# A hybrid attention and scan layer: six convolution blocks moved into the paired products, small roots and decay rows moved to GpSimd

## The chip, the cores and the metric

The kernel runs on one core of one Trainium2 chip. The metric is the device time of one execution in microseconds (us); lower is better. The engines are TensorE (PE; PEld is its loading of weights), VectorE (DVE), ScalarE (ACT), GpSimd (POOL) and SyncE (SP), which here only issues transfers. Each engine has a queue of its own and works through it in order.

## The reference

It is one layer of a streaming encoder, in float32, for 1024 tokens of a new stream and 64 tokens of a running one (512 cached keys): a shared input projection of width 1024, a short causal convolution and a chunked state scan (32 heads, 4 groups), a differential attention (8 heads of 2 components) beside it, gates, an output projection, and a convolutional feed-forward part of width 2816.

```python
xn = _rmsnorm(x, p['norm_mix_w'])
proj = xn @ p['w_in']
z, xbc, dt_raw, q, k, v, gate_ssm, gate_att = jnp.split(proj, np.cumsum(IN_SIZES)[:-1].tolist(), axis=-1)
xbc_c, conv_new = _causal_dwconv(conv_past, xbc, p['ssm_conv_w'], p['ssm_conv_b'])
xbc_c = jax.nn.silu(xbc_c)
...
y_ssm, ssm_new = _ssd_scan(xs, dt, a_neg, bm, cm, ssm_past.reshape(b, G, E, P, N), chunk_len)
y_ssm = (y_ssm + p['ssm_d'].reshape(G, E)[..., None] * xs).astype(x.dtype).reshape(b, t, SSM_D_INNER)
y_ssm = y_ssm * jax.nn.silu(z)
...
o = _diff_attention(q, k, v, q_pos, k_pos, lam)
o = (_rmsnorm(o, p['subln_w']) * (1.0 - lambda_init)).reshape(b, t, ATT_V_WIDTH)
mix = jax.nn.sigmoid(gate_ssm) * (y_ssm @ p['w_branch_ssm']) + jax.nn.sigmoid(gate_att) * (o @ p['w_branch_attn'])
x = x + mix @ p['w_out']
h = _rmsnorm(x, p['norm_ffn_w']) @ p['w_up']
ha, hb = jnp.split(h, 2, axis=-1)
hc, ffn_new = _causal_dwconv(ffn_past, ha, p['ffn_conv_w'], p['ffn_conv_b'])
x = x + (jax.nn.silu(hc) * hb) @ p['w_down']
```

The two places inside that the change touches are these, from the attention and from the scan:

```python
p = jax.nn.softmax(s, axis=-1).reshape(b, ATT_HEADS, 2, nq, -1)
a = p[:, :, 0] - lam * p[:, :, 1]
...
acum = jnp.cumsum(dtc * a_neg, axis=1)
seg = acum[:, :, None] - acum[:, None, :]
decay = jnp.exp(jnp.where(causal[None, :, :, None, None], seg, -jnp.inf))
```

## The kernel before

All 1088 tokens lie along the free axis, in two halves of 544 and quarters of 272; features lie on the 128 partitions. A float32 product is made from three fast ones: each operand is split into a rounded part (hi) and the rest (lo), and hi times hi, lo times hi and hi times lo are added up in PSUM. The weights are split when they arrive: ScalarE writes hi, VectorE subtracts (L156 and L157 for plain blocks, L429 and L430 for paired ones).

A **plain block** is 128 output features, made by `project`: four chunks of 272 tokens, each 8 slices of the inner dimension times 3 products (L171 to L173). A **pair** is two blocks and all tokens, made by `in_pair` with 7 products of half-size matrices in place of 8: each has 2 quarters x 4 slices x 3 matmuls of 272 columns. The left factors (`left_parts`, `make_left`; sums of weight blocks on GpSimd, L573 among them) and the right ones (`parts`, sums of token halves) are made ahead. The 7 products pile up in PSUM banks, and ScalarE or VectorE move a pile out, VectorE by adding `u1` or `u2` (L710). `INPUT` is the order of the pairs: q and k, z, then four of the gates g; `done` treats each finished half row and sends it to memory.

The stages follow each other:
1. A start with the norm and the values, to 116 us of the span.
2. The **stage of pairs**, 20 pairs, to 554 us. Other work (rotations of q and k, the step sizes) runs beside it as generators of small jobs, which `take_turn` advances.
3. **Attention**, to 1104 us: 8 heads x 9 query tiles = 72 units of `attend`. Each unit has two score products (psc banks), reductions, two exponentials with sums (L1142), the inversion of the second sum (L1144) and its product with lambda and the first sum (L1145), one multiply-add of the two probability tiles (L1146), transposes (L1157), copies to SBUF, and the product with the values. After 9 units `head_out` normalises the head with a logarithm and an exponential on ScalarE. Between them `fill(ATT_STEPS)` puts in chunks of `stream()`, the plain blocks of `ORDER`: the convolution blocks (`conv_tiles`: four taps, of which L1019 is three, and a silu made from tanh, L1020 and L1021) and gates. One unit of the rate is 363 columns, and `settle(1)` keeps one unit open: the scores of the next unit stand ahead of the transposes of this one.
4. The **scan**, to 1476 us: 36 steps over 4 groups of 9 chunks. `ask` fetches the decay rows of a step, spread over 128 partitions, into a `bc` tile (4 of them), two steps ahead; `front` masks it on GpSimd (L1317), applies exponentials and a product; `back` multiplies and carries the state (GpSimd, L1345). The rest of `stream()` and the two first branch products fill in between, with side loads through `b_g` tiles (`BG` of them).
5. The last branch and the output projection, to 1684 us, and the feed-forward part, to the end.

The code states the order of most work, and a scheduler turns it into queues: `tc.issue_after` keeps an instruction behind another, `tc.high_priority(n)` lets one go ahead. A tile of a pool with n buffers waits until the tile n before it is no longer used.

Of the kernel before, what the change touches and what calls it, by code (L numbers as in the profile page):

```python
# [17 lines left out]
P = 128  # L18
# [33 lines left out]
BG = 8  # L52
# [18 lines left out]
ATT_STEPS = 1.12  # L71
# [4 lines left out]
def group(g):  # L76
    return 16 + g, 20 + g, *range(4 * g, 4 * g + 4)


ORDER = (("c", group(0)), ("g", (11, 10)), ("c", group(1)), ("g", (9, 8)), ("c", group(2)), ("c", group(3)), ("g", (3, 2)))  # L80
INPUT = [(k, i) for k in "qk" for i in range(4)] + [("z", i) for i in range(8)] + [("g", i) for i in (2, 3, 6, 7)]
# [9 lines left out]
def hybrid_layer(ctx: ExitStack, tc: tile.TileContext, xT, xt, prm, cst, rope, wvd, win, wbs, wba, wout, wup, wdn,  # L91
# [239 lines left out]
    def staged(name):  # L331
        return st.tile([P, 384], F32, name=name, tag="zr", bufs=ZR)
# [153 lines left out]
    def row(tag, name, dt=F32):  # L486
# [3 lines left out]
        w = {"ss": T}.get(tag, HT)  # L490
        return rows_r.tile([P, w], dt, name=name, tag=tag, bufs=IN_ROWS[tag])
# [128 lines left out]
    def blocks_of(n):  # L620
        kind, j = INPUT[n]
        return [win[FIRST_BLOCK[kind] + 2 * j + r] for r in range(2)]
# [23 lines left out]
    def in_pair(n):  # L646
# [16 lines left out]
        def to(r, c, s):  # L663

            if (r, c) not in out:
                out[r, c] = row("fp", "pre")
            a, w = O2[s], W2[s]
            return out[r, c][:, a : a + w]

        def done(r, c):  # L670
            cs = slice(HT * c, HT * (c + 1))
# [22 lines left out]
        for _ in range(14):  # L694
# [8 lines left out]
            else:  # L703
# [3 lines left out]
                if u is None:  # L707
                    seen["copy"] = S.copy(to(r, c, s), ps)
                else:
                    seen["read"] = V.tensor_tensor(out=to(r, c, s), in0=ps, in1=u[:, us], op=ALU.add)  # L710
# [340 lines left out]
    with (tc.tile_pool(name="ak", bufs=1) as ak, tc.tile_pool(name="at", bufs=1) as at,  # L1051
# [51 lines left out]
        def attend(h, i, tiles, o_t, ssq, s0):  # L1103
# [40 lines left out]
            V.reciprocal(sm[:n, 1:2], sm[:n, 0:1])  # L1144
            V.scalar_tensor_tensor(sm[:n, 1:2], sm[:n, 1:2], nlam[:n], s0[:n, i : i + 1], ALU.mult, ALU.mult)  # L1145
# [33 lines left out]
            act(po[:n, P : 2 * P], po[:n, :P], AF.Square, accum_out=ssq[:n, i : i + 1])  # L1179
            yield  # L1180

        def head_out(h, o_t, ssq, s0):
            ms, rs, t0, t1 = (at.tile([P, 9], F32, name=n, tag=n, bufs=2) for n in ("ms", "ors", "on0", "on1"))
            V.tensor_tensor(out=ms, in0=s0, in1=s0, op=ALU.mult)
            V.tensor_scalar(ms, ms, EPS * 128, None, ALU.mult)
            V.tensor_tensor(out=ms, in0=ms, in1=ssq, op=ALU.add)
            act(t0, ms, AF.Ln, scale=1.0 / 128)
            act(t0, t0, AF.Exp, scale=-0.5)
# [813 lines left out]
```

## Time and profile before

| | |
|---|---|
| timed, median of 3 runs | 2409.57 us (2406.24 to 2413.95) |
| profiled execution | 2400.86 us |
| its span, first to last record | 2399.1 us |
| mean granted clock | 0.998 |
| ScalarE, activations of the exponentials L1142 | x144, 106.0 us |
| transfers | 450.58 MB, mean 188 GB/s |

Busy time by stage, in us of VectorE, ScalarE, GpSimd and TensorE (attention and the scan are among the rows of the prediction):

| stretch of the span, us | TensorE | VectorE | ScalarE | GpSimd |
|---|---|---|---|---|
| 0 to 116, start and values | 111.97 | 64.49 | 61.19 | 0.20 |
| 116 to 554, pairs | 434.78 | 315.29 | 199.18 | 142.36 |
| 1476 to 1590, a branch | 112.62 | 73.67 | 46.03 | 0.00 |
| 1684 to 2154, feed-forward, up | 466.60 | 329.46 | 191.21 | 226.12 |
| 2154 to 2399.1, feed-forward, down | 236.70 | 175.92 | 95.21 | 97.78 |

The profiled execution's own time is below the fastest of the timed runs; it is one execution, and its trace is what all durations come from. A row of a group gives a line of the kernel, the engine, the operation, what it writes and reads, its shape and count, then its busy time and mean duration, and at the end the idle time of its engine just before, with what ended it. Rows of stretches give the busy time of each engine between two times of the span. The weights of a matmul load beside the matmul before it, so PEld's busy time isn't added to PE's.

### The profile page before, as it was taken

The page shows a single profiled execution, that of the slowest core. Times are in us where ns is not written, and L with a number is a line of the kernel's source. Part 1 is how long each engine was busy: PE and PEld are TensorE (multiplying, and loading weights), DVE is VectorE, ACT ScalarE, POOL GpSimd, SP SyncE. Part 2 cuts the span into 40 slices and gives each one's busy share as a digit, 9 for nine tenths or more (in the row PEclk, how much of TensorE's full clock was granted, in tenths as well). Part 3 has the DMA queues.
Part 4 walks back from the last instruction along what each step waited for, and adds up shares of the span by engine and source line. Part 5 has one row for each costly group of instructions (what it writes and reads, how often), then busy time and mean ns, then how long its engine had stood idle before and what let it go on. Part 6 is the DMA issues. An engine that isn't in the chain of part 4 may idle for free.

```text
span 2399.1 us, 48662 instructions
## 1 busy us (share of the span) xinstructions
PE 2376.1 (99%) x18661; PEld 2306.1 (96%) x18661; DVE 1725.5 (72%) x2953; ACT 1197.8 (50%) x2592; POOL 623.0 (26%) x683
## 2 busy tenths in 40 slices
PE   9999999999999999999999999999999999999999
PEld 9999999999999999999899889999999999999999
DVE  4678987646858768884789886646866766767866
ACT  6344454425656656665666674334533443353432
POOL 0032444220100000001222220013254554453343
PEclk9999999999999999999999999999999999999999
DMA  7873868426555444435988956664124424357975
GB/s 248 273 243 135 275 214 310 165 105 205 158 160 161 148 141 138 143 114 183 360 272 287 333 192 207 197 211 139 63 82 159 148 96 160 124 182 220 253 189 120
DMA packets 288202, 450.58 MB, mean 188 GB/s; under 512 B 35865, under 2 KB 178082, under 8 KB 287970
## 3 DMA queue, kind: packets, MB, share of 16 engines
q1 hardware_dynamic: 259058, 388.39, 49.0%
q0 software_dynamic: 10176, 25.50, 5.0%
q10 hardware_dynamic: 18736, 33.59, 3.9%
q8 instruction: 147, 2.41, 0.4%
q14 instruction: 85, 0.70, 0.1%
HBM read 294.86 MB, written 152.50 MB: 186 GB/s over the span
## 4 chain that ended last, share of the span: by engine, by line
PE 56%; DVE 3%; DMA 1%; issue 1%; ACT 1%; SPq 0%; DVEq 0%; ACTq 0%
PE mx L1639 13%; PE mx L1821 6%; PE mm L1639 5%; PE mm L171 4%; PE mm L173 4%; PE mm L172 4%; PE mx L173 3%; PE mx L171 3%; PE mx L172 3%; PE mm L1821 2%; PE yi L1328 1%; PE stp L1340 1%; PE ye L1334 1%; PE po L1177 1%; PE tr L1307 1%
## 5 line engine op out<-in xcount | busy, mean ns | idle before, releaser
L171 PE MATMUL mm<-b,w_hi 128*128 128x272 f32 x1376 | 409.2, 297 | 0.0
L173 PE MATMUL mm<-b,w_lo 128*128 128x272 f32 x1376 | 404.0, 294 | 0.0
L172 PE MATMUL mm<-b,w_hi 128*128 128x272 f32 x1376 | 403.8, 294 | 0.0
L171 PEld LDWEIGHTS mm<-b,w_hi 128*128 128x128 f32 x1376 | 259.4, 188 | 7.2 <-issue 4.9
L172 PEld LDWEIGHTS mm<-b,w_hi 128*128 128x128 f32 x1376 | 259.4, 189 | 6.2 <-issue 4.9
L173 PEld LDWEIGHTS mm<-b,w_lo 128*128 128x128 f32 x1376 | 258.9, 188 | 3.9 <-issue 3.1
L1639 PE MATMUL mx<-m,w_hi 128*128 128x272 f32 x776 | 149.3, 290 | 1.5 <-ACT m L429 1.3
L430 DVE TENSOR_TENSOR wh<-w_f,wh 128x512 fp32r<-128x512 f32 (+1 forms) x156 | 149.1, 956 | 0.0
L1639 PE MATMUL mx<-n,wh 128*128 128x272 f32 x1056 | 141.2, 288 | 1.2 <-DVE u L1666 1.2
L1639 PEld LDWEIGHTS mx<-n,wh 128*128 128x128 f32 x1056 | 135.7, 188 | 1.4 <-DVE u L1666 1.4
L1142 ACT ACTIVATE p_t<-sc,mx 128x512 f32<-128x512 f32 (+6 forms) x144 | 106.0, 739 | 58.7 <-DVE mx L1133 35.0
L171 PE MATMUL mx<-b,w_hi 128*128 128x272 f32 x416 | 122.5, 295 | 1.6 <-ACT w_hi L156 1.1
L1639 PEld LDWEIGHTS mx<-m,w_hi 128*128 128x128 f32 x776 | 121.9, 188 | 2.0 <-ACT m L429 1.5
L172 PE MATMUL mx<-b,w_hi 128*128 128x272 f32 x416 | 122.0, 294 | 0.0
L173 PE MATMUL mx<-b,w_lo 128*128 128x272 f32 x416 | 120.1, 291 | 0.2 <-DVE w_lo L157 0.2
L573 POOL TENSOR_TENSOR ws<-w_f 128x512 f32<-128x512 f32 (+1 forms) x51 | 69.2, 1356 | 195.0 <-DMA w_f<-in_win_dram 94.0
L1019 DVE SCALAR_TENSOR_TENSOR cc<-pre,par,cc 128x544 f32<-128x544 f32 (+1 forms) x144 | 111.2, 772 | 8.2 <-ACT cc L1017 6.9
L157 DVE TENSOR_TENSOR w_lo<-w_f,w_hi 128x1024 fp32r<-128x1024 f32 (+1 forms) x74 | 91.1, 1232 | 31.3 <-ACT w_hi L156 30.7
L1639 PE MATMUL mx<-m,w_lo 128*128 128x272 f32 x388 | 112.0, 289 | 0.0
L1648 ACT ACTIVATE cc<-pre,par 128x544 f32<-128x544 f32 (+1 forms) x44 | 37.2, 845 | 148.0 <-DVE pre L1683 147.0
L429 ACT CAST wh<-w_f 128x512 fp32r<-128x512 f32 (+1 forms) x156 | 95.3, 613 | 28.7 <-POOL w_f L579 7.9
L156 ACT CAST w_hi<-w_f 128x1024 fp32r<-128x1024 f32 (+1 forms) x74 | 77.5, 1049 | 51.5 <-PE mm L172 28.4
(472 smaller groups left out, 7123.4 us busy)
## 6 DMA issues: line engine op xcount, KB each, us to landing
w_f<-in_win_dram SPq DMA_DIRECT2D x40, 512.0 KB, 3.6
w_f<-in_wup_dram SPq DMA_DIRECT2D x80, 256.0 KB, 2.6
w_f<-in_win_dram SPq DMA_DIRECT2D x76, 256.0 KB, 3.2
bc<-a_sc SPq DMA_DIRECT2D x32, 512.0 KB, 6.7
b<-y_sc SPq DMA_DIRECT2D x24, 544.0 KB, 9.3
h_sc<-hb SPq DMA_DIRECT2D x44, 272.0 KB, 2.1
ht<-h_sc SPq DMA_DIRECT2D x22, 544.0 KB, 4.7
t_sc<-ht SPq DMA_DIRECT2D x22, 544.0 KB, 2.9
```

Source lines behind the costliest of these rows:

```text
L156: S.copy(hi, w)
L157: V.tensor_tensor(out=lo, in0=w, in1=hi, op=ALU.subtract)
L171: PE.matmul(ps, a_hi, b_hi, start=i == 0, stop=False)
L172: PE.matmul(ps, a_hi, b_lo, start=False, stop=False)
L173: PE.matmul(ps, a_lo, b_hi, start=False, stop=i == n - 1)
L429: S.copy(hi, src)
L430: V.tensor_tensor(out=lo, in0=src, in1=hi, op=ALU.subtract)
L573: G.tensor_tensor(out=s1, in0=q21, in1=q22, op=ALU.add)
L1019: V.scalar_tensor_tensor(cc[:, :m], pre[:, i : i + m], cw(i), cc[:, :m], ALU.mult, ALU.add)
L1142: act(p_t[:n, :nk], sc[c][:n, :nk], AF.Exp, bias=mx[:n, c : c + 1], accum_out=dst)
L1639: PE.matmul(ps, w[x][:, c], b[y][:, k], start=start and k == i == 0, stop=k == 3 and i == 2, skip_group_check=not start)
L1821: PE.matmul(ps, w[y][:, c], b[z][:, k], start=start and k == j == 0, stop=k == n - 1 and j == 2, skip_group_check=not start)
```

## The change

- **Pairs.** The convolution blocks 16, 20, 0, 1, 2 and 3 leave `ORDER` and become three pairs of kind "c" in `INPUT`, behind z6, z7 and the first gate. `to` places their halves in longer rows (`fx`, `fc`: 3 more columns at each side), so that one evacuation of a quarter becomes two where the two streams meet. A new generator, `convolved`, does for each half row what `conv_tiles` does (ScalarE the first tap, VectorE three), then one Silu on ScalarE, and sends the result from ScalarE's queue; it joins `running`, the jobs that `take_turn` advances. `ATT_STEPS` goes from 1.12 to 0.87.
- **Roots and inversions.** The inversion of the sum becomes a power of -1 on GpSimd, and its product with lambda and the first sum follows there. In `head_out` the sums and a power of -0.5 on GpSimd replace VectorE's steps and ScalarE's logarithm and exponential; the factor of 128 goes into `wsub`. The Square reads the copied output and writes a tile of its own.
- **Decay rows.** `ask` issues its transfer from GpSimd in place of SyncE. The tiles of `side` and `staged` are 272 columns wide in place of 384, and `BG` goes from 8 to 12.

```diff
-BG = 8
+BG = 12
...
-ATT_STEPS = 1.12
+ATT_STEPS = 0.87
...
-ORDER = (("c", group(0)), ("g", (11, 10)), ("c", group(1)), ("g", (9, 8)), ("c", group(2)), ("c", group(3)), ("g", (3, 2)))
-INPUT = [(k, i) for k in "qk" for i in range(4)] + [("z", i) for i in range(8)] + [("g", i) for i in (2, 3, 6, 7)]
+PAIRED = ((16, 20), (0, 1), (2, 3))
+ORDER = (("c", group(1)), ("g", (11, 10)), ("c", group(2)), ("g", (9, 8)), ("c", group(3)), ("g", (3, 2)))
+INPUT = [(k, i) for k in "qk" for i in range(4)] + [("z", i) for i in range(6)]
+INPUT += [("z", 6), ("c", 0), ("z", 7), ("c", 1), ("g", 2), ("c", 2)] + [("g", i) for i in (3, 6, 7)]
...
     def staged(name):
-        return st.tile([P, 384], F32, name=name, tag="zr", bufs=ZR)
+        return st.tile([P, QW], F32, name=name, tag="zr", bufs=ZR)
...
-    def row(tag, name, dt=F32):
+    def row(tag, name, dt=F32, more=False):
         if tag in ("fa", "fs", "fu"):
             w = {"fa": KT * P, "fs": 4 * P, "fu": HT}[tag]
             return rows_l.tile([P, w], dt, name=name, tag=tag, bufs=IN_ROWS[tag])
-        w = {"ss": T}.get(tag, HT)
-        return rows_r.tile([P, w], dt, name=name, tag=tag, bufs=IN_ROWS[tag])
+        w = {"ss": T, "fx": HT + 6, "fc": HT + 6}.get(tag, HT)
+        t = rows_r.tile([P, w], dt, name=name, tag=tag, bufs=IN_ROWS[tag])
+        return t if tag == "ss" or more else t[:, :HT]
...
     def blocks_of(n):
         kind, j = INPUT[n]
+        if kind == "c":
+            return [win[B_X + f] for f in PAIRED[j]]
         return [win[FIRST_BLOCK[kind] + 2 * j + r] for r in range(2)]
...
         def to(r, c, s):
             if (r, c) not in out:
-                out[r, c] = row("fp", "pre")
-            a, w = O2[s], W2[s]
-            return out[r, c][:, a : a + w]
+                out[r, c] = row("fx" if kind == "c" else "fp", "pre", more=kind == "c")
+            a, w, d = O2[s], W2[s], 3 if kind == "c" else 0
+            if kind == "c" and c == 1 and s == 1:
+                m = TP - HT - a
+                return [(0, out[r, c][:, d + a : d + a + m]), (m, out[r, c][:, d + a + m + 3 : d + a + w + 3])]
+            return [(0, out[r, c][:, d + a : d + a + w])]
+
+        def convolved(r, c):
+            t, f = out[r, c], PAIRED[j][r]
+            n, m = (HT, HT) if c == 0 else (TP - HT, HT + 3)
+            if c == 0:
+                G.memset(t[:, 0:3], 0.0)
+            else:
+                G.tensor_copy(t[:, 0:3], out[r, 0][:, HT : HT + 3])
+                G.tensor_copy(t[:, 3 + n : 6 + n], par[:, O_CS + 3 * f : O_CS + 3 * f + 3])
+                G.tensor_copy(conv_o[:, f, 0:3], t[:, n : n + 3])
+                G.tensor_copy(conv_o[:, f, 3:6], t[:, HT + 3 : HT + 6])
+            cc = row("fc", "cc", more=True)
+            cw = lambda i: col(O_CW + 4 * f + i)
+            with after("copy"):
+                act(cc[:, :m], t[:, :m], AF.Identity, bias=col(O_CB + f), scale=cw(0))
+            yield 1
+            for i in range(1, 4):
+                with after("read"):
+                    V.scalar_tensor_tensor(cc[:, :m], t[:, i : i + m], cw(i), cc[:, :m], ALU.mult, ALU.add)
+                yield 1
+            with after("root", "copy"):
+                seen["silu"] = act(cc[:, :m], cc[:, :m], AF.Silu, scale=2.0)
+            yield 1
+            rs = slice(P * f, P * (f + 1))
+            send(out=x_sc[rs, HT * c : HT * c + n], in_=cc[:, :n])
+            if c == 1:
+                send(out=x_sc[rs, TP:T], in_=cc[:, n + 3 : m])
         def done(r, c):
+            if kind == "c":
+                for x in {(0, 0): (0,), (1, 0): (0, 1), (0, 1): (1,), (1, 1): ()}[r, c]:
+                    running.append([1 + 3 * (r == 1 and x == 1), convolved(r, x)])
+                return
...
                 ps = pile(key, p, s, start)
-                if u is None:
-                    seen["copy"] = S.copy(to(r, c, s), ps)
-                else:
-                    seen["read"] = V.tensor_tensor(out=to(r, c, s), in0=ps, in1=u[:, us], op=ALU.add)
+                for o, t in to(r, c, s):
+                    w = t.shape[1]
+                    if u is None:
+                        seen["copy"] = S.copy(t, ps)
+                    else:
+                        seen["read"] = V.tensor_tensor(out=t, in0=ps[:, o : o + w], in1=u[:, O2[s] + o : O2[s] + o + w], op=ALU.add)
...
                 pr.append(p_t)
-            V.reciprocal(sm[:n, 1:2], sm[:n, 0:1])
-            V.scalar_tensor_tensor(sm[:n, 1:2], sm[:n, 1:2], nlam[:n], s0[:n, i : i + 1], ALU.mult, ALU.mult)
+            G.tensor_tensor(out=sm[:n, 1:2], in0=sm[:n, 0:1], in1=minus[:n, 9:10], op=ALU.pow)
+            G.tensor_scalar(sm[:n, 1:2], sm[:n, 1:2], nlam[:n], s0[:n, i : i + 1], ALU.mult, ALU.mult)
...
                 PE.matmul(po[:n, :P], a_t[b // 4][:kw, b % 4 * P : b % 4 * P + n], rhs, start=b == 0, stop=b == nb - 1)
             S.copy(o_t[:n, i], po[:n, :P])
-            act(po[:n, P : 2 * P], po[:n, :P], AF.Square, accum_out=ssq[:n, i : i + 1])
+            sq = at.tile([P, P], F32, name="sq", tag="sq")
+            act(sq[:n], o_t[:n, i], AF.Square, accum_out=ssq[:n, i : i + 1])
             yield
         def head_out(h, o_t, ssq, s0):
-            ms, rs, t0, t1 = (at.tile([P, 9], F32, name=n, tag=n, bufs=2) for n in ("ms", "ors", "on0", "on1"))
-            V.tensor_tensor(out=ms, in0=s0, in1=s0, op=ALU.mult)
-            V.tensor_scalar(ms, ms, EPS * 128, None, ALU.mult)
-            V.tensor_tensor(out=ms, in0=ms, in1=ssq, op=ALU.add)
-            act(t0, ms, AF.Ln, scale=1.0 / 128)
-            act(t0, t0, AF.Exp, scale=-0.5)
-            V.tensor_scalar(ms, ms, -0.5 / 128, None, ALU.mult)
-            V.tensor_tensor(out=ms, in0=ms, in1=t0, op=ALU.mult)
-            V.tensor_tensor(out=t1, in0=ms, in1=t0, op=ALU.mult)
-            V.scalar_tensor_tensor(rs, t1, 1.5, t0, ALU.add, ALU.mult)
+            ms, rs = (at.tile([P, 9], F32, name=n, tag=n, bufs=2) for n in ("ms", "ors"))
+            G.tensor_tensor(out=ms, in0=s0, in1=s0, op=ALU.mult)
+            G.tensor_scalar(ms, ms, EPS * 128, None, ALU.mult)
+            G.tensor_tensor(out=ms, in0=ms, in1=ssq, op=ALU.add)
+            G.tensor_tensor(out=rs, in0=ms, in1=minus[:, :9], op=ALU.pow)
             V.tensor_tensor(out=o_t[:, :8], in0=o_t[:, :8], in1=rs[:, :8].unsqueeze(2).to_broadcast([P, 8, P]), op=ALU.mult)
...
-        V.tensor_scalar_mul(wsub, par[:, O_SUB : O_SUB + P], 1.0 - LAMBDA_INIT)
+        V.tensor_scalar_mul(wsub, par[:, O_SUB : O_SUB + P], (1.0 - LAMBDA_INIT) * math.sqrt(128.0))
+        minus = at.tile([P, 10], F32, name="minus")
+        V.memset(minus, -0.5)
+        V.memset(minus[:, 9:10], -1.0)
...
             ch, h8 = (c + o) // P, slice(8 * g, 8 * g + 8)
             L = P if ch < 8 else TS
             bc = sin.tile([P, 8, P], F32, name="bc", tag="bc", bufs=4)
-            load(out=bc[:, :, :L], in_=a_sc[ch, h8, :L].unsqueeze(0).to_broadcast([P, 8, L]))
+            G.dma_start(out=bc[:, :, :L], in_=a_sc[ch, h8, :L].unsqueeze(0).to_broadcast([P, 8, L]))
             return bc
...
         def side():
-            return bs.tile([P, 384], F32, name="b_g", tag="b_g", bufs=BG)
+            return bs.tile([P, QW], F32, name="b_g", tag="b_g", bufs=BG)
```

In the stage of pairs, these are rows of VectorE at the last quarter of one pair and the start of the next, before (`mx` and `mm` are banks, `u1` and `u2` the running sums, `pre` the row of a result, `wh` and `w_lo` split left factors):

```order
L710 TENSOR_TENSOR pre_6637<-mx_6624,u1_6458 128x272
L710 TENSOR_TENSOR pre_6637<-mm_6641,u1_6458 128x272
L430 TENSOR_TENSOR wh_6655<-ws2_6588,wh_6655 128x512
L710 TENSOR_TENSOR pre_6670<-mx_6590,u2_6459 128x272
L430 TENSOR_TENSOR wh_6674<-w_f_1759,wh_6674 128x512
L710 TENSOR_TENSOR pre_6670<-mx_6609,u2_6459 128x272
L430 TENSOR_TENSOR wh_6690<-w_f_1758,wh_6690 128x512
L430 TENSOR_TENSOR w_lo_6712<-ws1_6587,w_hi_6711 128x512
```

After, the same place behind the first convolution pair:

```order
L751 TENSOR_TENSOR pre_6983<-mx_6900,u2_6767 128x272
L432 TENSOR_TENSOR wh_6985<-w_f_1759,wh_6985 128x512
L751 TENSOR_TENSOR pre_6983<-mx_6920,u2_6767 128x208
L751 TENSOR_TENSOR pre_6983<-mx_6920,u2_6767 128x64
L432 TENSOR_TENSOR wh_7005<-w_f_1758,wh_7005 128x512
L695 SCALAR_TENSOR_TENSOR cc_6989<-pre_6950,par_81,cc_6989 128x544 x2
L432 TENSOR_TENSOR w_lo_7026<-ws1_6896,w_hi_7025 128x512
L695 SCALAR_TENSOR_TENSOR cc_6989<-pre_6950,par_81,cc_6989 128x544
L695 SCALAR_TENSOR_TENSOR cc_7035<-pre_6983,par_81,cc_7035 128x547
L432 TENSOR_TENSOR w_lo_7026<-w_f_1759,w_hi_7025 128x512
L739 TENSOR_TENSOR u2_7010<-mx_7063,u1_7009 128x272
```

The evacuation at the seam of the two streams is two instructions, and the taps of the convolution (L695) stand among the splits (L432) and ahead of the next pair's evacuation (L739).

In attention, these are rows of VectorE where a unit of 1024 keys is followed by one of 128 keys (`sm` holds a unit's sums, `sc` the scores' bank, `mx` the maxima, `p_t` the probabilities, `pt` transposes), before:

```order
L1144 RECIPROCAL sm_10664<-sm_10664 128x1
L1145 SCALAR_TENSOR_TENSOR sm_10664<-sm_10664,nlam_7211,s0_10570 128x1
L1136 MEMSET sc_10752 64x2x64
L1146 SCALAR_TENSOR_TENSOR p_t_10682<-p_t_10682,sm_10664,p_t_10680 128x1024
L1137 TENSOR_REDUCE mx_10751<-sc_10752 128x2
L1144 RECIPROCAL sm_10750<-sm_10750 128x1
L1145 SCALAR_TENSOR_TENSOR sm_10750<-sm_10750,nlam_7211,s0_10570 128x1
L1146 SCALAR_TENSOR_TENSOR p_t_10761<-p_t_10761,sm_10750,p_t_10759 128x128
```

After, at such a place:

```order
L1173 MEMSET sc_11876 64x64
L1174 TENSOR_REDUCE mx_11868<-sc_11876 128x1
L1177 MEMSET sc_11943 64x2x64
L1187 SCALAR_TENSOR_TENSOR p_t_11885<-p_t_11885,sm_11867,p_t_11883 128x1024
L1178 TENSOR_REDUCE mx_11942<-sc_11943 128x2
L1205 COPY a_t_11820<-pt_11819 128x4x64
L1207 COPY a_t_11827<-pt_11826 64x64
L1173 MEMSET sc_12013 64x64
L1174 TENSOR_REDUCE mx_12012<-sc_12013 128x1
L1187 SCALAR_TENSOR_TENSOR p_t_11952<-p_t_11952,sm_11941,p_t_11950 128x128
```

The inversions and products have left, and the multiply-add (L1187) of a unit now stands behind the reduction of the unit after it. GpSimd's rows at this place, which before has none of these lines:

```order
L1185 TENSOR_TENSOR sm_11867<-sm_11867,minus_8012 128x1
L1186 TENSOR_SCALAR sm_11867<-sm_11867,nlam_8024,s0_11800 128x1
L1185 TENSOR_TENSOR sm_11941<-sm_11941,minus_8012 128x1
L1186 TENSOR_SCALAR sm_11941<-sm_11941,nlam_8024,s0_11800 128x1
L1228 TENSOR_TENSOR ms_11890<-ms_11890,ssq_10997 128x9
L1229 TENSOR_TENSOR ors_11891<-ms_11890,minus_8012 128x9
```

Each unit adds a power (L1185) and a product (L1186), and each head the rows of `head_out` between them.

In the scan, these are rows of GpSimd over some steps, before (`bc` holds the decay rows, `state` the state):

```order
L1345 TENSOR_TENSOR state_14349<-state_14272,decs_95 128x512
L1317 AFFINE_SELECT bc_14165<-bc_14165 128x1024
L1345 TENSOR_TENSOR state_14461<-state_14349,decs_95 128x512
L1345 TENSOR_TENSOR state_14608<-state_14461,decs_95 128x512
L1317 AFFINE_SELECT bc_14274<-bc_14274 128x1024
L1345 TENSOR_TENSOR state_14692<-state_14608,decs_95 128x512
L1317 AFFINE_SELECT bc_14352<-bc_14352 128x1024
```

After:

```order
L1385 TENSOR_TENSOR state_14368<-state_14291,decs_95 128x512
L1334 DMA bc_14293<-a_sc_77 128x1024
L1385 TENSOR_TENSOR state_14480<-state_14368,decs_95 128x512
L1334 DMA bc_14371<-a_sc_77 128x1024
L1385 TENSOR_TENSOR state_14627<-state_14480,decs_95 128x512
L1334 DMA bc_14551<-a_sc_77 128x1024
L1334 DMA bc_14630<-a_sc_77 128x1024
L1385 TENSOR_TENSOR state_14745<-state_14627,decs_95 128x512
L1357 AFFINE_SELECT bc_14293<-bc_14293 128x1024
L1385 TENSOR_TENSOR state_14834<-state_14745,decs_95 128x512
```

Each step's transfer (L1334) now stands in GpSimd's queue between the state's products (L1385), ahead of masks (L1357) of earlier steps.

## The prediction

> **What bounds the kernel now.** I read the page's head first, then the busy times stage by stage, then the waits of TensorE, and last the cadence of its matmuls.
>
> ```profile
> span 2399.1 us, 48662 instructions
> PE 2376.1 (99%) x18661; PEld 2306.1 (96%) x18661; DVE 1725.5 (72%) x2953; ACT 1197.8 (50%) x2592; POOL 623.0 (26%) x683
> ```
>
> ```profile
> core 0: us, PE busy (x) PEld busy (x) DVE busy (x) ACT busy (x) POOL busy (x), PEclk, DMA share, GB/s
> 231.00:350.00 119.00, 118.66 (x925) 117.06 (x925) 104.26 (x172) 66.11 (x125) 48.77 (x45) 1.00 0.67 224
> 350.00:554.00 204.00, 203.59 (x1615) 203.13 (x1614) 123.21 (x214) 78.77 (x149) 60.20 (x52) 1.00 0.57 198
> 554.00:1104.00 550.00, 548.10 (x4213) 526.46 (x4213) 414.09 (x817) 336.80 (x863) 43.39 (x120) 1.00 0.47 149
> 1104.00:1476.00 372.00, 371.38 (x3007) 334.31 (x3006) 296.32 (x396) 228.34 (x550) 84.90 (x68) 1.00 0.80 272
> ```
>
> The first two rows are the stage of pairs after its start, the third is attention, the fourth the scan. TensorE is busy in all of them, with a full granted clock. A busy share of modelled ends isn't proof, so the next two views decide. These are rows of the waits of TensorE, of the whole span first, then of attention and the scan (us in total, times, longest):
>
> ```profile
> PE mm L659 <- ACT t L429: 1.6, 2, 1.0
> ...
> PE pw L1222 <- DVE s L1257: 1.3, 1, 1.3
> PE sc L1128 <- ACT p_t L1142: 0.5, 1, 0.5
> ...
> PE mx L171 <- ACT grs L1365: 0.5, 1, 0.5
> ```
>
> The longest total of the whole span is 1.6 us, and attention and the scan together have 2.3 us. The cadence (pairs' matmuls alone, plain blocks, the FFN's pairs):
>
> ```profile
> 460.00:500.00 40.00, 40.00 (x320) 40.00 (x319) 1.00 0.31 107
> ...
> 1520.00:1550.00 30.00, 30.00 (x240) 1.00 0.61 186
> ...
> 1850.00:2100.00 250.00, 250.00 (x1991) 1.00 0.38 133
> ```
>
> A matmul of 272 columns starts every 250/1991 = 0.1256 us in the longest stretch, and 40/320 and 30/240 give 0.125 for a pair's matmul and a plain block's alike. No stretch is faster. So the number of matmuls sets the time, and every other engine matters only if it makes TensorE wait.
>
> **Part 1: six blocks as three pairs.** A plain block is 4 chunks x 8 x 3 = 96 matmuls; six are 576, all taken from the filler of attention. A pair is 7 products x 2 halves x 4 x 3 = 168; three are 504, added behind z5 in the stage of pairs. The difference is 72 matmuls: 72 x 0.1256 = **9.0 us off**. By stage: attention loses 576 x 0.1256 = 72.3 us (550 to about 478), the pairs gain 504 x 0.1256 = 63.3 us. The rate falls from 1.12 to 0.87 of 363 columns per unit, so 72 units take 72 x 0.25 x 363/272 = 24 chunks less, which is six blocks x 4: what is left for the scan is the same.
>
> The weights are the same bytes. The convolutions move with the blocks:
>
> ```profile
> L1019 DVE SCALAR_TENSOR_TENSOR cc<-pre,par,cc 128x544 f32<-128x544 f32 x72 | 55.6, 773 | 7.0 <-ACT cc L1017 6.3 <-issue 0.2
> L1019 DVE SCALAR_TENSOR_TENSOR cc<-pre,par,cc 128x547 f32<-128x547 f32 x72 | 55.6, 772 | 1.2 <-ACT cc L1017 0.6
> ...
> L157 DVE TENSOR_TENSOR w_lo<-w_f,w_hi 128x1024 fp32r<-128x1024 f32 x29 | 35.4, 1220 | 14.8 <-ACT w_hi L156 14.6
> ...
> L1021 DVE SCALAR_TENSOR_TENSOR cc<-pre,cc 128x547 f32<-128x547 f32 x24 | 17.2, 716 | 2.9 <-ACT pre L1020 2.9
> ```
>
> VectorE gets 36 x 0.773 = 27.8 us of them in the stage of pairs, on top of what a pair needs anyway (123.2 us over 204/21.1 = 9.7 pairs, 12.7 a pair). From z6 on there are nine pairs, 9 x 21.1 = 190 us, with 9 x 12.7 + 27.8 = 142 us of VectorE: 75%. The stretch 231 to 350 ran with 104.26/119 = 88% and TensorE idle for 0.34 us, so the matmuls hide this work; if that cover failed once in each of the three convolution pairs, as at the 1.3 us wait for s above, it would cost 3 x 1.3 = 4 us. What is queued behind a convolution step on VectorE is the evacuation of a bank. I take **+0.5** of 0 to 4, near the crowded row.
>
> Attention loses 36 x (0.773) + 12 x 0.716 + 6 x 1.220 = 43.7 us of VectorE. It had 414.09 in 550, and has 370 in 478: 77% after 75%. No relief there, and hardly more pressure.
>
> **Part 2: roots and inversions on GpSimd.** Rows of the removed operations (attention):
>
> ```profile
> L1145 DVE SCALAR_TENSOR_TENSOR sm<-sm,nlam,s 128x1 f32<-128x1 f32 x64 | 13.7, 214 | 1.5
> ...
> L1144 DVE RECIPROCAL sm<-sm 128x1 f32<-128x1 f32 x64 | 10.2, 160 | 25.5 <-ACT p_t L1142 25.1
> ```
>
> ```profile
> L1187 ACT ACT_TABLE_LOAD x7 | 9.0, 1283 | 0.1
> L1188 ACT ACT_TABLE_LOAD x7 | 9.0, 1283 | 0.1
> ```
>
> VectorE loses 0.160 + 0.214 = 0.37 us a unit (27 us in 72; it brings attention back to 343/478 = 72%) and 25 us of standing at the reciprocal; ScalarE loses 18 us of table loads. Neither was waited for by TensorE, so I book nothing for them; nor for the Square, which now reads the copied output and so lets go of its bank one step earlier. Added is a hop: exponential, power, product, then L1146. No power on GpSimd is in this trace. The nearest rows are its copies of three elements, beside VectorE's instruction of that moment:
>
> ```profile
> 1000.49 0.18 POOL L1014 COPY conv_o<-pre 128x3 f32<-128x3 f32 x1
> ```
>
> ```profile
> 983.23 1.19 POOL L1014 COPY conv_o<-pre 128x3 f32<-128x3 f32 x1
> ```
>
> ```profile
> 980.65 0.15 DVE L1144 RECIPROCAL sm<-sm 128x1 f32<-128x1 f32 x1
> ...
> 981.95 1.29 DVE L1146 SCALAR_TENSOR_TENSOR p_t<-p_t,sm 128x1024 f32<-128x1024 f32 x1
> 983.16 1.22 DVE L157 TENSOR_TENSOR w_lo<-w_f,w_hi 128x1024 fp32r<-128x1024 f32 x1
> ```
>
> ```profile
> 985.26 0.60 PE L1157 MATMUL pt<-con,p_t 128*128 128x128 f32 x4
> ```
>
> The same copy takes 0.18 us alone and 1.19 beside L157, and ends with it (984.42 and 984.38). So two small operations cost between 0.36 and 2.4 us, less the 0.37 removed: 0 to 2 us later. A power may cost more than a copy, and no row here says how much; I take 1 us a hop, the stretched copy's length less what VectorE no longer does. The unit quoted, with L1146 done at 983.24 and its first transpose at 985.26, had 2.0 us to spare. The order shows that L1146 now stands behind a reduction of the next unit, so VectorE doesn't stand still meanwhile, and that on average 82 matmuls of 272 columns lie between a unit's last score and its first transpose, where 66 did: 16 x 0.1256 = 2.0 us more cover against 0 to 2 us more chain. What would be late next is the next unit's scores, since exponentials free their banks (the 0.5 us row above), and behind L1146 stand reductions that these exponentials wait for. I take **+0.5** of -1.8 (the two attention waits gone) to +36 (0.5 us in each unit).
>
> The Trainium skill speaks against this part: its page "SBUF — State Buffer", section "Who interferes with whom", says that a VectorE instruction with two SBUF inputs and a GpSimd instruction that reads SBUF exclude each other for a whole instruction. The two copies above agree with it. By that rule the convolutions and L1146 can stand in front of each power and product, and GpSimd in front of them; it is the mechanism of the second rival.
>
> **Part 3: decay rows issued by GpSimd, 12 buffers.** SP loses 36 issues and GpSimd gains them. The rows (the scan's tile bc; then transfers of about the same size from both queues, KB and median us to landing):
>
> ```profile
> L1294 SPq DMA_DIRECT2D bc<-a_sc x36: 319/402/2101, 1113.4 to 1426.3; - x36
> ...
> DMA to landing us min/median/max: 3.3/6.7/12.8
> ```
>
> ```profile
> w_f<-in_wup_dram SPq DMA_DIRECT2D x80, 256.0 KB, 2.6
> ...
> x<-k_r POOLq DMA_DIRECT2D x16, 272.0 KB, 5.9
> ```
>
> ```profile
> L845 POOL DMA_DIRECT2D x<-k_r x12 | 6.6, 550 | 30.8 <-DVE u L700 8.4 <-ACT pre L676 7.8 <-DVE ss L259 7.5
> ```
>
> GpSimd's busy time in the scan rises from 84.9 by 36 x 0.55 = 20 us, of 372. Rows may land 5.9 - 2.6 = 3.3 us later. An issue waits until the row four steps back is used, and on GpSimd the mask of another step and the state's product stand behind it. A step is 372/36 = 10.3 us, and requests are two steps ahead, so 3.3 us fit. SP no longer stands at these issues, but nothing on SP was waited for by TensorE, nor the side loads that the four more buffers serve. I take **0** of -0.5 (the one wait of the scan) to +12 (a third of the steps 1 us late).
>
> **Sum.** -9.0 + 0.5 + 0.5 + 0 = -8.0 us. The profiled execution took 2400.86 us (span 2399.1 and 1.8 around it), so 2392.9. The timed runs' median is 2409.57, 8.7 us above it and with a spread of 7.7 us; nothing in the profile says what these 8.7 us are, so I carry the difference over: 2409.57 - 8.0 = **2401.6 us**.
>
> **Rivals.**
> 1. *No change*: attention's own chain takes the place of the matmuls. Its period falls from 550/72 = 7.64 to 6.64 us a unit while scores, reductions and exponentials stay; 9.0/72 = 0.125 us of waiting for a bank per unit eats all. For it: the only bank wait of attention is just this one. Against: it is 0.5 us in 72 units, and VectorE's share falls. Between 0.05 and 0.12 us a unit: 2404 to 2410. Chance 0.22.
> 2. *Slower*: GpSimd's hop comes after the transposes' turn. TensorE takes its queue in order, so each late unit stops everything. It decides once the hop exceeds the spare time, about 2 us in the quoted unit plus 2 of new cover. If a third of the 72 units come 1 us late, +24 us: 2409.6 - 9 + 24 = 2425; it turns the sign at 9 us, an eighth of the units. For it: the stretched copy, and the unknown power. Against: the cover grew. Chance 0.12.
> 3. *The scan pays*: a mask waits on GpSimd behind an issue and rows land late; +8 to +12 us, 2409 to 2413. For it: 3.3 us to landing. Against: two steps of lead. Chance 0.08.
> 4. *More*: the hidden relief counts after all and the small waits go too (2.3 us of attention and scan, 2 to 4 us elsewhere): -13 to -15, 2395 to 2397. Against: TensorE waited for none of it. Chance 0.08.
>
> **How the numbers follow.** The forecast, 2398 to 2406, has 0.50. A measurement tells about 0.3%, 7.2 us, from no change: below 2402.3 is faster. Four fifths of the forecast and rival 4 are there: 0.40 + 0.08 = 0.48. A fifth of the forecast, rival 1 and half of rival 3 are within: 0.10 + 0.22 + 0.04 = 0.36. Rival 2 and the other half of 3 are 0.16. The range leaves out rival 2's long end and, with some 3 us for the spread of the runs, goes from 2393 to 2417.
>
> **What would show it.** 3864 pair matmuls and 5952 of plain blocks at 0.1256 us; the stage of pairs ending near 554 + 63 = 617, attention lasting near 478, the scan 372; TensorE's waits still a few us. L1157's counterpart waiting for the scaled probabilities shows rival 2, scores waiting for exponentials rival 1, yi or the mask waiting for bc rival 3. The prediction is wrong if the cadence changes, or if power costs several us.

## The result and the profile after

The changed kernel took 2420.88 us (median of 5 runs, 2416.55 to 2426.35) beside 2409.42 us for the kernel before; the ratio is 1.0052, 95% interval [1.0037, 1.0067]. The forecast was 2401.6 us, 8 us less than before, with a range of 2393 to 2417; the result lies above the range, and the change makes the kernel slower. A second series of the same kernel (e13) gave 2415.45 us, by itself just inside the range, and 1.0035 [1.0022, 1.0049], so it is slower too. The head of the changed kernel's page, and its busy times by stage (the end of the pairs, attention, the scan):

```profile
span 2415.6 us, 48453 instructions
PE 2375.3 (98%) x18589; PEld 2303.5 (95%) x18589; DVE 1719.8 (71%) x2794; ACT 1184.4 (49%) x2559; POOL 767.3 (32%) x907
```

```profile
554.00:617.70 63.70, 63.70 (x508) 63.70 (x508) 36.08 (x61) 24.24 (x45) 13.81 (x11) 1.00 0.37 125
617.70:1108.00 490.30, 486.73 (x3702) 464.33 (x3702) 345.07 (x573) 293.63 (x782) 131.35 (x264) 1.00 0.50 155
1108.00:1482.00 374.00, 362.92 (x2923) 325.70 (x2922) 293.72 (x387) 224.81 (x539) 114.32 (x106) 0.99 0.81 269
```

TensorE has 72 instructions less, and still 2375 us of work; what stands out is the scan, where it is idle for 374.00 - 362.92 = 11.1 us. Where the time went is clearer with the stages cut at the same instructions in both kernels: the last matmul of the pairs, the last product with the values (po), 3 us behind the last norm of the scan (gst), the first matmul of the feed-forward part's up half, and the last of its down half. "Idle" is the sum of the gaps between TensorE's records, in us:

| stretch | before, length (idle) | after, length (idle) |
|---|---|---|
| start and pairs | 554.1 (6.1) | 617.7 (6.7) |
| attention | 557.9 (1.9) | 493.6 (3.6) |
| scan | 364.0 (0.6) | 372.7 (11.1) |
| branch and output | 208.3 (1.4) | 210.0 (1.1) |
| feed-forward, up and down | 709.5 (6.6) | 716.2 (11.2) |

The pairs took 63.6 us more, as forecast (63.3). Attention and scan together fell by 55.6 us in place of 72.3. The feed-forward part isn't changed; its idle time was 6.8 us in the second profile of the same kernel, and it lasted 709.5 to 715.2 us in the profiles of the other runs, so I put that difference down to the execution. The waits of TensorE in attention, then in the scan, follow. (`pt` are the banks of attention's transposes and of the product with the values, `po` and `o_t` stand for emptying that product, `ol` for emptying a head's output. In the scan, `tr` and `cb` are the first matmuls of a step, `yi` and `ye` those of its result, `stp` the one for the state, and `gst` is the sum for a norm.)

```profile
PE pt L1198 <- DVE ol L1243: 1.3, 1, 1.3
PE pw L1262 <- DMA q<-q_st: 1.1, 1, 1.1
PE pt L1198 <- ACT o_t L1219: 0.6, 1, 0.6
```

```profile
PE gst L1402 <- DVE zin L1398: 3.6, 1, 3.6
PE cb L1349 <- ACT b_cb L1352: 3.2, 2, 1.7
PE tr L1347 <- DMA in<-x_sc: 2.8, 1, 2.8
PE mm L173 <- ACT w_hi L158: 1.0, 1, 1.0
```

And the stretches around three of these waits, with the granted clock third from the end:

```profile
1070.00:1080.00 10.00, 8.10 (x54) 7.64 (x53) 7.50 (x14) 5.20 (x14) 2.06 (x6) 0.83 0.31 112
...
1120.00:1130.00 10.00, 7.19 (x46) 6.97 (x46) 2.68 (x3) 2.71 (x4) 0.00 (x0) 0.83 0.58 180
...
1470.00:1480.00 10.00, 6.40 (x49) 6.21 (x48) 7.66 (x10) 3.04 (x4) 0.00 (x0) 0.97 0.50 173
1480.00:1490.00 10.00, 9.48 (x52) 8.55 (x52) 3.60 (x7) 3.42 (x6) 0.00 (x0) 0.69 0.36 95
```

These waits are paid twice: behind them the clock stays down for a while. 10 us at 0.83 lose 1.7 us, and the four rows lose 1.7 + 1.7 + 0.3 + 3.1 = 6.8 us, 1.1 of them past the cut at 1484.0. With 12.1 us more idle (14.7 for 2.5) that is 17.8 us up to the cut, for 16.7 us missing in attention and scan. The Trainium skill, "TensorE: Matmul & The Clock Gate", "What's actually happening", gives half clock until one busy window of about 3.4 us has passed; an estimate from this is a loss of 3.4/2 = 1.7 us, and the rows at 0.83 agree. It asks for an idle window of 3.4 us first, and here the measurement decides: 0.6 and 1.3 us of gaps close together were enough at 1075.

### The profile page after: what moved, and what is told of

It reads as the page before. It is cut to its first block, busy times and chain, and to the rows that moved or that the text cites. A ratio compares the mean times of both kernels' runs of the same rounds, so it can differ in the third digit from the quotient of the medians.

```text
span 2415.6 us, 48453 instructions
## 1 busy us (share of the span) xinstructions
PE 2375.3 (98%) x18589; PEld 2303.5 (95%) x18589; DVE 1719.8 (71%) x2794; ACT 1184.4 (49%) x2559; POOL 767.3 (32%) x907
## 4 chain that ended last, share of the span: by engine, by line
PE 82%; DMA 6%; DVE 6%; issue 3%; ACT 1%; POOL 1%; SPq 0%; DVEq 0%; POOLq 0%; ACTq 0%
PE mx L1679 12%; PE mx L664 11%; PE mm L173 6%; PE mm L175 6%; PE mm L174 6%; PE mx L1861 5%; PE mm L1679 5%; PE mm L664 5%; PE mx L173 4%; PE mx L174 4%; PE mx L175 4%; PE po L1218 3%; PE mm L1861 2%; PE sc L1169 2%; PE sc L1170 2%
## 5 line engine op out<-in xcount | busy, mean ns | idle before, releaser
L173 PE MATMUL mm<-b,w_hi 128*128 128x272 f32 x1184 | 352.4, 298 | 1.0 <-ACT w_hi L158 1.0
L175 PE MATMUL mm<-b,w_lo 128*128 128x272 f32 x1184 | 349.9, 296 | 0.0
L174 PE MATMUL mm<-b,w_hi 128*128 128x272 f32 x1184 | 348.1, 294 | 0.0
L173 PEld LDWEIGHTS mm<-b,w_hi 128*128 128x128 f32 x1184 | 223.2, 189 | 7.2 <-issue 4.1
L174 PEld LDWEIGHTS mm<-b,w_hi 128*128 128x128 f32 x1184 | 223.3, 189 | 6.4 <-issue 5.0
L175 PEld LDWEIGHTS mm<-b,w_lo 128*128 128x128 f32 x1184 | 223.0, 188 | 5.0 <-issue 4.1
L432 DVE TENSOR_TENSOR wh<-w_f,wh 128x512 fp32r<-128x512 f32 (+1 forms) x165 | 154.6, 938 | 0.0
L576 POOL TENSOR_TENSOR ws<-w_f 128x512 f32<-128x512 f32 (+1 forms) x54 | 74.3, 1376 | 227.4 <-DMA w_f<-in_win_dram 100.2
L431 ACT CAST wh<-w_f 128x512 fp32r<-128x512 f32 (+1 forms) x165 | 100.8, 613 | 26.3 <-POOL w_f L582 5.7
L1185 POOL TENSOR_TENSOR sm<-sm,minus 128x1 f32<-128x1 f32 (+1 forms) x72 | 44.6, 620 | 211.4 <-ACT p_t L1183 211.1
L578 POOL TENSOR_TENSOR w_f<-w_f,ws 128x512 f32<-128x512 f32 (+1 forms) x54 | 79.6, 1474 | 100.1 <-issue 55.7
L1696 POOL TENSOR_TENSOR hb<-hb,cc 128x544 f32<-128x544 f32 (+2 forms) x63 | 66.5, 1069 | 134.0 <-DVE hb L1717 99.5
```

What stands on the lines that cost most here:

```text
L173: PE.matmul(ps, a_hi, b_hi, start=i == 0, stop=False)
L174: PE.matmul(ps, a_hi, b_lo, start=False, stop=False)
L175: PE.matmul(ps, a_lo, b_hi, start=False, stop=i == n - 1)
L431: S.copy(hi, src)
L432: V.tensor_tensor(out=lo, in0=src, in1=hi, op=ALU.subtract)
L576: G.tensor_tensor(out=s1, in0=q21, in1=q22, op=ALU.add)
```

## The experiments

Each ratio is to the kernel before in the same job; "idle" is that of attention and scan, cut as above.

| run | what it is | median, us | ratio [95%] | idle, attention / scan |
|---|---|---|---|---|
| e13 | changed kernel again | 2415.45 | 1.0035 [1.0022, 1.0049] | 2.7 / 10.8 |
| e1 | rows back on SyncE | 2409.64 | 1.0010 [1.0001, 1.0019] | 2.7 / 6.2 |
| e2 | roots back on VectorE and ScalarE | 2430.46 | 1.0093 [1.0079, 1.0107] | 8.4 / 14.7 |
| e3 | before + pairs and rate | 2423.39 | 1.0072 [1.0058, 1.0086] | 7.3 / 9.6 |
| e4 | before + rows on GpSimd | 2416.54 | 1.0046 [1.0034, 1.0059] | 2.5 / 8.0 |
| e5 | first three rows on SyncE | 2410.84 | 1.0015 [1.0006, 1.0023] | 3.9 / 7.6 |
| e6 | e1 + more matmuls at the scan's end | 2400.82 | 0.9976 [0.9967, 0.9984] | 2.8 / 2.6 |
| e7 | e3, filler moved from scan to attention | 2445.26 | 1.0157 [1.0144, 1.0170] | 1.6 / 34.2 |
| e8 | before + roots on GpSimd | 2411.92 | 1.0018 [1.0007, 1.0030] | 1.7 / 6.9 |
| e9 | changed kernel + scan's end | 2405.05 | 0.9987 [0.9976, 0.9998] | 4.5 / 5.7 |
| e10 | e5 + scan's end | 2404.62 | 0.9989 [0.9978, 1.0000] | 3.3 / 4.5 |
| e11 | e6 without the roots | 2409.65 | 1.0005 [0.9996, 1.0014] | 8.4 / 5.5 |
| e12 | before + scan's end | 2407.07 | 0.9993 [0.9984, 1.0003] | 2.4 / 2.1 |
| e14 | e6 without the side buffers | 2404.26 | 0.9993 [0.9983, 1.0003] | 4.6 / 4.7 |
| e15 | e1 with rate 0.92 | 2427.45 | 1.0094 [1.0075, 1.0113] | 3.3 / 20.0 |

**The decay rows.** e1 and e4 undo them and make them alone; e5 gives back only the first three.

```diff
-            G.dma_start(out=bc[:, :, :L], in_=...)
+            load(out=bc[:, :, :L], in_=...)                                            # e1
+            (load if c + o < 3 * P and g == 0 else G.dma_start)(out=bc[:, :, :L], in_=...)  # e5
```

> The changed kernel with the decay rows issued by SyncE again, all else as changed. Theory Q (the queue of the decay rows costs the scan about 10 us): TensorE's gaps of 2.8 us at the first tr, of 1.7 and 1.5 us at cb go, the 3.6 us gap at the last gst stays; the time falls by 6 to 10 us to 2411 to 2415, about 2 to 6 us above before. Theory P (the pairs' part alone costs it): nothing moves, 2418 to 2424. Theory N (the gaps come and go by themselves): gaps of the same sum at other places, 2417 to 2424.

> The kernel before with the decay rows issued by GpSimd alone. Theory Q: slower by 6 to 12 us, 2415 to 2421, with a gap of 2 to 3 us at the first tr and gaps over 1 us at cb. If Q is wrong: within 3 us of before.

> The changed kernel, but the first three decay rows of the scan are issued by SyncE, behind the scan's first load; all later rows stay with GpSimd. Theory Q1 (most of the rows' price is the start of the scan, where rows from a second queue land beside the first load): the gap of 2.8 us at the first tr goes with its slower clock, and the time falls by 4 to 7 us, to 2414 to 2417. Theory Q2 (the price is spread over all steps, since each issue stands between masks and products on GpSimd): the gap goes, the time falls by less than 3 us, 2418 to 2423.

Alone the rows cost 0.46%, some 11 us; undone (e1) they give back 6 to 10 us, by the ratio's distance from 1.0035 and from 1.0052. e5 gives back 5 to 9 of these, so the start of the scan carries most of the price and the steps little. The transfers issued there, by SyncE and GpSimd in the changed kernel, and by SyncE before:

```profile
1111.28 0.80 SPq L1321 DMA_DIRECT2D in<-x_sc  x2
1112.13 0.42 SPq L1322 DMA_DIRECT2D in<-x_sc  x1
```

```profile
1111.56 2.26 POOL L1334 DMA_DIRECT2D bc<-a_sc  x4 [18.15 <-PE po L1218]
```

```profile
1112.09 0.80 SPq L1281 DMA_DIRECT2D in<-x_sc  x2
1112.93 0.42 SPq L1282 DMA_DIRECT2D in<-x_sc  x1
1113.40 0.50 SPq L1294 DMA_DIRECT2D bc<-a_sc  x1
...
1124.56 0.90 SPq L1294 DMA_DIRECT2D bc<-a_sc  x2
```

Before, one row follows the scan's first load and the next two come 11 us later; GpSimd, free at that moment, issues four at once, 512 KB each, beside the load. Times to landing of the load's last transfer (L1322 now, L1282 before; the longest is the third number):

```profile
DMA to landing us min/median/max: 5.6/7.4/11.1
```

```profile
DMA to landing us min/median/max: 5.7/7.7/8.7
```

It is the first one that took 11.1 us, and tr waited 2.8 us for it; the first one before took 6.0 us, and tr didn't wait. Every profile bears this out. In the five kernels with all rows on GpSimd (the changed one, e13, e2, e4, e9) this transfer took 10.7 to 12.1 us and tr waited 2.4 to 3.9; in the ten that issue the first rows from SyncE and start the scan in the same way (all others but e7 and e15) it took 6.0 to 7.2 us, and tr waited 0.4 at most. The waits further on are less clear: the scheduler also gives the scan another order with each of these edits, and with it other small waits, so the rest of the 11 us isn't placed.

**The scan's end.** In the order of TensorE's queue, 73 matmuls stand between the last step (stp) and the last norm (gst) before, and 49 in the changed kernel.

```diff
             with tc.high_priority(LAST):
                 gated(*due)
+            yield i
+            with tc.high_priority(LAST):
                 scaled(*due, normed(*due))
```

> The kernel of e1 (decay rows on SyncE, pairs, roots on GpSimd) with one more turn of the filler between the last step of the scan and its norm: 108 matmuls between the last stp and the last gst in place of 60. Theory E (the scan's end waits because too few matmuls stand there): the gap of 2.8 us at gst and the slower clock behind it (some 3 us) go, 2403 to 2406, and it is faster than before. If the wait only moves to the branch behind the scan: 2407 to 2411.

> The changed kernel with one more turn of the filler at the scan's end (97 matmuls between the last stp and the last gst in place of 49). Theory E: the gap of 3.6 us at gst and the slower clock behind it go, 6 to 9 us less, 2411 to 2415; the first rows' price of some 10 us stays. If it lands above 2417, the scan's end is not a cause of its own.

> The changed kernel with both mends, the first three rows from SyncE and one more turn of the filler at the scan's end (90 matmuls there). If the two prices add up, 2421 - 10 - 8 = 2401 to 2404, faster than before by 3 to 7 us. If they are one price counted twice, 2408 to 2411.

> The kernel before with one more turn of the filler at the scan's end (95 matmuls in place of 73). It waits only 0.5 us there, so no change: 2404 to 2410. If it gains 4 us or more, e6's gain is not from the wait at gst.

TensorE at this place, in the changed kernel and in e6:

```profile
1468.63 1.12 PE L1380 MATMUL stp<-xx,b_cb 64*128 64x512 f32 x2
1479.60 1.40 PE L1402 MATMUL gst<-zin,con 128*128 128x320 f32 x2 [3.60 <-DVE zin L1398]
```

```profile
1463.28 1.12 PE L1380 MATMUL stp<-xx,b_cb 64*128 64x512 f32 x2
1478.06 0.70 PE L1402 MATMUL gst<-zin,con 128*128 128x320 f32 x2
```

The wait and its slow clock are gone, and e6 is faster than the kernel before, the best of all. The same edit does nothing for the kernel before (e12), which waited 0.1 us at gst. The count isn't the only thing that matters there. From the end of stp to the norm's input (zin), VectorE and ScalarE took 9.2 us before and 9.7 in the changed kernel, but 7.9 in e5, which waits 1.8 us with the same 49 matmuls, and 14.1 in e14 (below), which waits 1.7 with 110 (12 of them yi and ye). On the changed kernel (e9) it gives 12 to 16 us by the ratios, more than the 6 to 9 expected; the two profiles differ by 8.5 us from the scan to the output (582.7 and 574.2), and the rest isn't placed. With the end mended, the first rows give nothing further (e10 to e9). This doesn't show that the two prices are one: in e10 the wait of 2.4 us at tr is gone, but a wait of 2.6 us at ye stands further on, which e9 doesn't have (e5 has it too), and in e4 the rows cost their 11 us in a kernel that waits 0.1 us at gst. Why e10 gains nothing stays open.

**The attention units and the roots.**

```diff
-ATT_STEPS = 0.87
-SCAN_STEPS = 1.17
+ATT_STEPS = 1.0              # e7
+SCAN_STEPS = 0.91            # e7
...
-            G.tensor_tensor(out=sm[:n, 1:2], in0=sm[:n, 0:1], in1=minus[:n, 9:10], op=ALU.pow)
-            G.tensor_scalar(sm[:n, 1:2], sm[:n, 1:2], nlam[:n], s0[:n, i : i + 1], ALU.mult, ALU.mult)
+            V.reciprocal(sm[:n, 1:2], sm[:n, 0:1])          # e2, e3, e7, e11, with the Square, head_out and wsub as before
+            V.scalar_tensor_tensor(sm[:n, 1:2], sm[:n, 1:2], nlam[:n], s0[:n, i : i + 1], ALU.mult, ALU.mult)
```

> The kernel before with the six blocks as three pairs and the rate 0.87 alone. By the sum of the prediction -8.5 us, 2401. Theory Q, with the scan's end late because of the pairs (49 matmuls between the last stp and the last gst where before has 73): the 3.6 us gap and a slow stretch of 3 us stay, so 2404 to 2408. Theory P: slower than before, 2412 to 2420.

> The kernel of e3 (pairs alone) with the filler's rate in attention 1.0 in place of 0.87 and in the scan 0.91 in place of 1.17: the same matmuls, some 37 us of them moved from the scan to attention. Theory C (the attention units wait because the lower rate leaves fewer matmuls between them): TensorE's waits at pt and sc in attention fall from 6.6 us to under 2 us, those of the scan rise by several us. Theory M (the waits come from what the pairs stage leaves behind, not from the rate): attention's waits stay over 5 us. The total is not what tells them apart, 2412 to 2430.

> The changed kernel with the reciprocal, its product and the root of head_out as before (VectorE and ScalarE), all else as changed. Theory R (the hop to GpSimd costs attention 3 us, a gap of 1.9 us near the end and its slower clock): 2417 to 2419 and no gap in attention over 0.5 us. Theory Q: no change within 3 us, 2418 to 2424, the scan's gaps stay; by Q the roots can even help, so up to 2426.

> The kernel before with the roots and inversions on GpSimd alone. Theory C (the hop helps only where attention is short of cover): within 3 us of before, 2404 to 2410. Theory R+ (less work on VectorE and ScalarE helps anywhere): 2397 to 2402. Rival 2 of the prediction: 2412 or more.

> The kernel of e6 with the roots and inversions on VectorE and ScalarE as before: pairs, more buffers and the mended scan's end. Theory C (the hop to GpSimd relieves the thin attention): attention's waits rise from 2.8 to 7 or 8 us again, the time to 2406 to 2411. If the roots did not matter: 2400 to 2403.

TensorE's waits in attention, in e3, then in e7, then in e6:

```profile
PE pt L1198 <- DVE ol L1247: 2.8, 2, 2.0
PE sc L1169 <- ACT p_t L1183: 2.1, 2, 1.6
PE pt L1198 <- ACT po L1220: 1.7, 3, 1.0
```

```profile
PE pw L1263 <- DMA q<-q_st: 1.6, 1, 1.6
```

```profile
PE pt L1198 <- DVE ol L1243: 1.3, 1, 1.3
PE pt L1198 <- ACT o_t L1219: 0.6, 1, 0.6
```

The pairs alone are slower than before by 0.7%. Of the 72.3 us of matmuls that left its attention and scan, 20.0 are missing: 5.4 are more waiting in attention, 9.0 more waiting in the scan (3.7 at gst), and the rest fits the lower clock (0.83 from 1080 to 1090, for one). In attention the rate of 0.87 leaves units that wait for the pt banks, which head_out's transposes and the product with the values fill just ahead of a unit's own, and for scores' banks. With the rate at 1.0 (e7) they wait no more, and the scan, which lost that filler, idles 34 us. So the rate causes attention's waits (theory C). The roots on GpSimd take most of them away, without more filler: from e11 to e6 the ratio falls by 0.0029, 7 us, for 5.6 us of idle time in attention and 3.0 in the scan; from e2 to the changed kernel by 10 to 14 us, some of it in the scan. But the edit of the Square goes with the roots in all these runs, and 1.7 us of e3's waits are for a bank that the Square still holds (po L1220). How much of the gain is the Square's wasn't tried. Alone (e8) they change nothing in attention; the 0.18% that they cost stand in the scan, whose idle time is 6.9 us in place of 0.6 although its code is the same. Its instructions come in another order there; which of them costs it wasn't tried. The hop itself is small:

```profile
L1185 POOL TENSOR_TENSOR sm<-sm,minus 128x1 f32<-128x1 f32 x64 | 39.3, 614 | 205.9 <-ACT p_t L1183 205.8
L1186 POOL TENSOR_SCALAR sm<-sm,nlam,s 128x1 f32<-128x1 f32 x64 | 29.1, 454 | 5.8
```

**What was open.** A second profile, the side buffers, and the rate as another way to mend the scan's end.

```diff
-BG = 12
+BG = 8                       # e14, with side and staged 384 wide
...
-ATT_STEPS = 0.87
+ATT_STEPS = 0.92             # e15
```

> The changed kernel once more, for a second profile. TensorE's waits in the feed-forward stages, whose code is the same, were 11.2 us in its first profile and 6.1 to 9.3 us in all others. If they are of the execution: 6 to 9 us this time. If they belong to the changed kernel: again over 10 us. The scan's waits (11.1 us, 3.6 of them at gst) should stand within 2 us in either case, and the time at 2417 to 2424.

> The kernel of e6 with the eight side tiles of 384 columns as before in place of twelve of 272. The prediction booked nothing for them: 2399 to 2403. If the larger ring of side loads carries a part of the gain (e1 less e3 is -14 us, of which the roots explain some 9): 2404 to 2407.

> The kernel of e1 with the rate 0.92 in place of 0.87 and no extra turn at the scan's end; by this alone 73 matmuls stand between the last stp and the last gst, as before. Theory E (only their number counts): the gst wait goes to under 1 us as in e6, 2400 to 2405. If e6's gain came from its other order: the wait stays over 2 us, 2407 to 2411.

e13 has the same waits at the same places (2.8 us at tr, 3.4 at gst), so these belong to the kernel. e14 stands at 0.9993 beside e6's 0.9976, about 4 us, with a wait of 1.7 us at gst; they ran in different jobs and their intervals just touch, so what the buffers are worth stays open. e15 missed: the wait at gst fell to 0.8 us, as theory E has it, but the ratio is 0.0084 above that of e1, 20 us. TensorE's waits of its scan:

```profile
PE cb L1349 <- ACT b_cb L1352: 2.5, 2, 2.1
PE yi L1368 <- DVE bc L1360: 2.5, 4, 1.1
PE mm L173 <- DMA b<-y_sc: 1.9, 1, 1.9
PE tr L1347 <- DVE xx L1356: 1.9, 3, 1.0
```

More filler in attention brings the branch that reads the scan's own result (y_sc) into the scan earlier: its first load is issued 164 us behind the last product with the values, in place of 182 in e1, and a matmul waits 1.9 us for it. The other 18 us are spread over the steps, which have less filler between them; they weren't traced to a cause one by one. The number of matmuls at one place can't be had by the rate alone.

## Why the prediction was wrong

- **Part 1, the count: right.** 504 matmuls in the stage of pairs took 63.6 us (63.3 forecast), and the convolutions there hid beside them (0.6 us more idle; 0 to 4 foreseen). Counted in the order of the two programs, attention lost 545 of the 576 matmuls up to its last product with the values, and the scan the other 31.
- **Part 1, "what is left for the scan is the same": the step that failed first.** By count it nearly holds (31 of some 2900 matmuls less). But what decides is where the filler stands: 49 matmuls in place of 73 at the scan's end are 24 x 0.1256 = 3.0 us less cover, the chain to the norm is 0.5 us longer, and the wait at gst is 3.6 us in place of 0.1. The rows of TensorE's order at that place show it, and the prediction doesn't speak of them. The parts of this sum, -9.0 + 0.5, came to some 17 us more when the pairs stood alone (e3), and mending this one place on the changed kernel gave 12 to 16 us (e9).
- **Part 3, "0 of -0.5 to +12": mis-sized.** Alone it cost some 11 us, near its upper end. The argument of two steps of lead is about the middle of the scan, where e5 leaves little to pay. At the start there is no lead: what SyncE's queue had kept apart, two queues issued at once, and the scan's first load took 11.1 us in place of 6.0. Rival 3 had the right stage and size, but neither the place nor the mechanism: it spoke of masks behind issues and of late rows, and it was the load beside the rows that came late.
- **Part 2, the hop: right in size, wrong in worth.** Power and product take 0.61 + 0.45 us for 0.37 removed, inside the bounds, and L1146's counterpart is not late; rival 2 didn't come. But "Neither was waited for by TensorE, so I book nothing for them" fails once the rate falls: with the pairs, the roots and the Square's edit together are worth 7 us or more.
- **Attention, +0.5 of -1.8 to +36: too low.** It fell by 64.3 us where 545 x 0.1256 = 68.5 us of matmuls left it. The added cover was counted between scores and transposes; the waits came at pt's two banks, where that count says nothing. So rival 1 came in a small form and at other banks: it had named the scores' banks, and those waits appear only without the roots (2.1 of the 8.4 us idle in e2).
- **Not in the sum at all:** the slower clock behind a wait, 1.7 us for two of these places and 3.4 at the scan's end.

So -9.0 us of matmuls stood against waits at three seams (the scan's start, its end, the heads' ends) and their clock; some 4 us more of waits inside the scan (cb, mm) belong to none of the three, and no run isolates them. With two of the seams mended, e6 is 0.24% faster than before.

## What to carry to other kernels

Where one engine is busy 99% and all others are hidden, taking filler out is taking cover out: look first at the seams, where a chain must finish before the next stage, and count the matmuls that stand there in the new order, not the sum over a stage. A transfer moved to another queue loses its place behind the transfers it used to follow, and the first step of a loop, which has no lead, pays for it. Small work moved off a crowded engine is worth what the next change makes of it, so parts are best timed alone and together: here the rows alone cost 11 us and the pairs alone 17, and the roots with the Square's edit, which cost 4 alone, were worth 7 or more beside the pairs.

## What the hardware showed unexpectedly

The granted clock can fall behind waits of 2 us, and the same wait doesn't always do it. e1 and e6 wait 1.9 us at the same instruction (stp L1380, for the state), up to 1370.5 and 1371.3. These are the stretches there, of e1, then of e6; the clock is third from the end:

```profile
1370.00:1380.00 10.00, 9.45 (x54) 8.42 (x55) 6.59 (x9) 4.70 (x9) 2.68 (x3) 0.83 0.77 272
```

```profile
1370.00:1380.00 10.00, 8.65 (x61) 7.51 (x61) 7.39 (x10) 6.16 (x11) 3.23 (x3) 1.00 0.89 321
```

In the same way, behind the wait of 2.0 us at pt near the end of attention the clock was 0.84 and 0.83 over 10 us in e2 and e3 and stayed full in e11. In the changed kernel the gaps of 1.7 us at 1199 and 1.0 at 1204 left it at full, and the two gaps of 0.6 and 1.3 us at 1075 did not.

With longer waits it stays down longer. These are stretches of e7 behind gaps of 2.4 us at 1150 and 6.7 us at 1154, with two of about 1 us at 1163 and 1168:

```profile
1150.00:1160.00 10.00, 1.73 (x8) 0.97 (x6) 1.69 (x3) 1.50 (x3) 0.00 (x0) 0.64 0.83 294
1160.00:1170.00 10.00, 6.26 (x22) 4.07 (x24) 3.68 (x3) 7.18 (x18) 2.87 (x3) 0.50 1.05 359
1170.00:1180.00 10.00, 9.48 (x60) 6.98 (x56) 5.89 (x7) 7.30 (x22) 4.60 (x4) 0.67 1.05 346
```

The lowest value is 0.50, and in these 30 us the share lost adds up to 3.6 + 5.0 + 3.3 = 11.9 us, as much as 23.8 us at 0.50. Some 10 us of this time TensorE waited anyway (12.5 us of gaps, of which the first 2.4 came ahead of the slow clock), and a slow clock costs nothing then. That leaves some 7 us lost on top of the gaps.
